# A two-layer attention and GLA trunk: other orders of sums, squares, copies and loads at the beginning, at the MLP starts and at the end of layer 0's attention

## The chip, the cores and the metric

The kernel runs on one core of a Trainium2 chip. The metric is the device time of one execution in microseconds (us). A core has a matrix engine (TensorE, PE in the profile, with its weight loads as PEld), a vector engine (VectorE, DVE), an activation engine (ScalarE, ACT), GpSimd (POOL) and a queue engine (SyncE, SP) that issues nearly all DMAs here. Every engine works off its own instructions strictly in the order in which the program lists them, and waits on semaphores for the others. So an order written in the program is an order of execution on that engine.

## The reference

Input and output are (1, 1024, 1024) float32: 1024 rows (S), width D = 1024, two layers.

```python
for i in range(DEPTH):
    h = rmsnorm(x, norm_mix_w[i])
    x = x + (dilated_attention if i == 0 else gla_mixer)(h, ...)
    h = rmsnorm(x, norm_mlp_w[i])
    x = x + sq_relu_mlp(h, mlp_w_up[i], mlp_w_down[i])     # relu(h @ w_up)**2 @ w_down, D_FF = 4096
return rmsnorm(x, final_norm_w)
```

Dilated attention has 8 heads of width 128 in three groups (window 128, 512, 2048; dilation 1, 4, 16), each group with its own q, k, v (h @ w_in, 9 x 1024 columns), rotary positions and a banded softmax; the three groups of a head are merged by their softmax denominators, and the merged rows go through w_out. GLA is chunked gated linear attention with 4 heads; the change does not touch it.

## The kernel before, in words

**Operands.** A float32 product is done by three matmuls in a reduced type: each operand x is cut into a high part h (an ACT copy) and a low part l = x - h (a DVE subtraction), and hi*hi, hi*lo, lo*hi are added in PSUM. A tile's name ends in h or l accordingly (`dh`/`dl`, `a12h`/`a12l`, `wgh`/`wgl`, `whi`/`wlo`).

**Seven products.** The large products (values, heads, up and down projections) split both matrices into 2 x 2 quarters and form seven products of quarters instead of eight. On the side of the activations, with a11, a12, a21, a22 the quarters of the transposed, normalised rows, the operands are a11, a12, a22, s1 = a21 + a22, s2 = s1 - a11, s3 = a11 - a21, s4 = a12 - s2. On the side of the weights they are quarters b and differences of them (tiles `t`, cut into `wb` and `wg`; `wa` and `wd` are plain quarters).

**Halves** (L338) makes the activations' operands from x: `norm` (row scale by `row_rstd`: ACT squares with a row sum, Ln and Exp on ACT with some small DVE steps; then `xn`, four or eight scalar_tensor_tensor steps on DVE), `turn` (PE transposes into a bank pT, ACT copies into the tile `a`), `sum1` to `sum4` (DVE), and `cut`/`split` (ACT copy, DVE subtraction). p = 0 to 3 is a block of 256 rows; c = 0, 1 is a half of an operand.

**The beginning** (from L1157) interleaves Halves with the first steps of `Values` (L700), which projects h onto v: step n has a `load`, a `prep` (perhaps a difference of weights, tile `kept`, then `dh` and `dl`), a `product` into four banks of pA or of pB, and `sums`, which empties banks (ACT copies `c<-pB`, DVE additions `c<-pA,c`). Steps 0 and 1 take a12 into pB, 2 and 3 a11 into pA, 4 and 5 s1 into pB, 6 and 7 s2 into pA, which needs pA emptied by `sums(4)` (blocks 0 and 1 of the four) and `sums(5)` (blocks 2 and 3). Two of the `dl` subtractions (`prep(0, pool)` and `prep(2, pool)`) run on POOL.

**The end of the attention** (from L1261): a queue of closures in time steps (`at(step, fn)`); the last head's scores (pS, on DVE and ACT the masked exponentials `pt`, the turned `pP`, the values `pO`) follow the last products of the head and run into the output projection. `follow` gives the steps at which each of the last heads' parts run, `tail` the merges of the last heads (`load`, `start`, `finish` make `om` from `rows`; `t_head` transposes them), `W.dma`/`W.prep` load and cut the output weights (`raw`, `whi`, `wlo`). `out_proj` (L1306) adds the projection to x block by block: a bank `pd` of 12 matmuls, then on DVE `xs<-pd,xs`; after each it advances the queue.

**The MLP start.** `out_proj` calls `Halves.middle` and `Halves.after` between its last blocks, then `Halves.finish` (L440), an order written out by hand of the up projection's products (`up.product(p, s)`) with everything else. `Up` (L520) has 16 pairs p of 256 columns; `load` brings a pair's weights, `stage(p, 0..6)` makes its operands, `done` reads a bank after its product and squares the result, `sums` forms what the down projection needs. s = 0 to 6 stands for a11, a12, s2, s1, s3, a22, s4. Banks X, Y, Z, V are shared: (p, s2) and (p, s3) add to X after (p, a11). From p = 2 or 3 on `Up.run` goes on in a regular order. Both layers have the same start.

## Time and profile before

| what | us |
|---|---|
| median of 3 runs | 2719.67 (2719.61 to 2720.84) |
| profiled execution, its own time | 2720.89 |
| its span in the profile | 2719.1 |
| PE busy | 2647.2 (97%) |
| DVE / ACT / POOL busy | 1790.9 / 1236.9 / 97.3 |
| mean granted PE clock | 0.991 |

The span is cut into stretches in the prediction: the beginning is 0 to 80 us, layer 0's attention ends and the output projection runs from 880 to 1004 us, layer 0's MLP starts at 1004 us and layer 1's at 2080 us. A row of the timeline gives start, duration, engine, line, operation, out<-in, shapes, count, and in brackets the idle time before it with what ended it. A row of the waits view gives the engine, what waited, for what, the total us, how many times and the longest.

### The profile page before, as it was taken

The page shows a single profiled execution, that of the slowest core. Times are in us where ns is not written, and L with a number is a line of the kernel's source. Part 1 is how long each engine was busy: PE and PEld are TensorE (multiplying, and loading weights), DVE is VectorE, ACT ScalarE, POOL GpSimd, SP SyncE. Part 2 cuts the span into 40 slices and gives each one's busy share as a digit, 9 for nine tenths or more (in the row PEclk, how much of TensorE's full clock was granted, in tenths as well). Part 3 has the DMA queues.
Part 4 walks back from the last instruction along what each step waited for, and adds up shares of the span by engine and source line. Part 5 has one row for each costly group of instructions (what it writes and reads, how often), then busy time and mean ns, then how long its engine had stood idle before and what let it go on. Part 6 is the DMA issues. An engine that isn't in the chain of part 4 may idle for free.

```text
span 2719.1 us, 33226 instructions
## 1 busy us (share of the span) xinstructions
PE 2647.2 (97%) x12248; PEld 2185.8 (80%) x12248; DVE 1790.9 (66%) x2938; ACT 1236.9 (45%) x2296; POOL 97.3 (4%) x74
## 2 busy tenths in 40 slices
PE   7999999999999898999999999999999899999998
PEld 5788888888888786888888887778888688888887
DVE  5744788888888667666656672562657766656567
ACT  5423355555555345555534343442425555553344
POOL 0000000000000000000000001321200000000000
PEclk9999999999999999999999999999999999999999
DMA  3542455655656533444775453012223444486543
GB/s 144 170 148 92 125 140 145 163 148 139 164 135 190 193 116 111 165 145 154 268 253 191 132 179 113 24 36 66 80 92 117 139 151 151 151 311 211 194 145 126
DMA packets 311412, 402.16 MB, mean 148 GB/s; under 512 B 18865, under 2 KB 183217, under 8 KB 311249
## 3 DMA queue, kind: packets, MB, share of 16 engines
q1 hardware_dynamic: 311248, 400.04, 46.6%
q8 instruction: 96, 1.57, 0.2%
q14 instruction: 68, 0.55, 0.1%
HBM read 267.13 MB, written 107.68 MB: 138 GB/s over the span
## 4 chain that ended last, share of the span: by engine, by line
PE 58%; DVE 6%; ACT 3%; issue 1%; DMA 0%; SPq 0%; DVEq 0%; ACTq 0%
PE pB L1439 13%; PE pA L1439 10%; PE pX L613 7%; PE pd L213 5%; PE pd L215 5%; PE pd L214 5%; PE pV L613 5%; PE pZ L613 2%; PE pY L613 2%; PE pT L263 1%; PE pO L1614 1%; PE pU L1600 0%; PE pO L1613 0%; PE pT L363 0%; ACT c L622 0%
## 5 line engine op out<-in xcount | busy, mean ns | idle before, releaser
L1439 PE MATMUL pB<-dh 128*128 128x512 f32 x512 | 199.4, 389 | 0.0
L1439 PE MATMUL pB<-dh,dl 128*128 128x512 f32 x512 | 199.2, 389 | 0.0
L1439 PE MATMUL pB<-dl,dh 128*128 128x512 f32 x512 | 199.2, 389 | 0.0
L222 DVE TENSOR_TENSOR dl<-sin,dh 128x1024 fp32r<-128x1024 f32 x112 | 136.6, 1220 | 43.4 <-ACT dh L219 42.8
L219 ACT ACTIVATE dh<-sin 128x1024 fp32r<-128x1024 f32 x112 | 117.8, 1052 | 89.2 <-PE pB L1439 38.6
L872 ACT ACTIVATE pt<-pt,orow 128x128 f32<-128x128 f32 (+1 forms) x192 | 85.0, 444 | 151.8 <-DVE orow L870 150.8
L613 PE MATMUL pV<-s4h,wd 128*128 128x512 f32 x448 | 152.1, 400 | 1.1 <-DVE rb L640 1.1
L219 ACT ACTIVATE dh<-kept 128x1024 fp32r<-128x1024 f32 x64 | 67.9, 1061 | 183.1 <-DVE kept L1404 137.8
L1439 PE MATMUL pA<-dh 128*128 128x512 f32 x384 | 149.4, 389 | 0.0
L1439 PE MATMUL pA<-dl,dh 128*128 128x512 f32 x384 | 149.4, 389 | 0.0
L1439 PE MATMUL pA<-dh,dl 128*128 128x512 f32 x384 | 149.4, 389 | 0.0
L551 DVE TENSOR_TENSOR wbl<-t,wbh 128x1024 fp32r<-128x1024 f32 x56 | 68.6, 1225 | 71.5 <-ACT wbh L550 71.5
L613 PE MATMUL pX<-s3h,wgh 128*128 128x512 f32 x224 | 94.8, 423 | 18.5 <-ACT wgh L550 11.9
L1439 PEld LDWEIGHTS pB<-dh,dl 128*128 128x128 f32 x512 | 96.1, 188 | 20.0
L1439 PEld LDWEIGHTS pB<-dl,dh 128*128 128x128 f32 x512 | 96.1, 188 | 19.9
L1439 PEld LDWEIGHTS pB<-dh 128*128 128x128 f32 x512 | 96.1, 188 | 19.8
L622 ACT ACTIVATE c<-c 128x512 f32<-128x512 f32 x64 | 40.5, 632 | 147.3 <-DVE c L632 97.2
L551 DVE TENSOR_TENSOR wal<-raw,wah 128x512 fp32r<-128x512 f32 (+1 forms) x108 | 76.1, 706 | 44.8 <-ACT wah L550 44.8
L148 POOL TENSOR_TENSOR wlo<-raw,whi 128x1024 fp32r<-128x1024 f32 x16 | 40.0, 2499 | 1759.1 <-ACT whi L147 1756.1
L613 PEld LDWEIGHTS pV<-s4h,wd 128*128 128x128 f32 x448 | 84.1, 188 | 20.5 <-DVE rb L640 2.8
L213 PE MATMUL pd<-whi,hTh 128*128 128x512 f32 x256 | 100.5, 393 | 0.0
L215 PE MATMUL pd<-whi,hTl 128*128 128x512 f32 x256 | 99.7, 389 | 0.0
(309 smaller groups left out, 7479.1 us busy)
## 6 DMA issues: line engine op xcount, KB each, us to landing
sin<-acts SPq DMA_DIRECT2D x112, 512.0 KB, 3.7
raw<-in_mlp_w_up_dram SPq DMA_DIRECT2D x64, 512.0 KB, 6.1
acts<-s SPq DMA_DIRECT2D x64, 512.0 KB, 3.3
raw<-in_mlp_w_down_dram SPq DMA_DIRECT2D x64, 512.0 KB, 4.6
raw<-in_attn_w_in_dram SPq DMA_DIRECT2D x96, 256.0 KB, 4.4
cw<-c SPq DMA_DIRECT2D x192, 128.0 KB, 2.3
acts<-c SPq DMA_DIRECT2D x64, 256.0 KB, 2.0
kept<-in_mlp_w_down_dram SPq DMA_DIRECT2D x32, 512.0 KB, 5.2
```

What stands on the lines that cost most here:

```text
L148: eng.tensor_tensor(lo, src, hi.bitcast(F32), op=OP.subtract)
L213: pe.matmul(ps, sh, mh, start=start, stop=False)
L214: pe.matmul(ps, sh, ml, start=False, stop=False)
L215: pe.matmul(ps, sl, mh, start=False, stop=stop)
L219: act.activation(hi, src, AF.Copy)
L222: dve.tensor_tensor(lo, src, hi.bitcast(F32), op=OP.subtract)
L263: pe.transpose(ps[:, k, 128 * i:128 * i + 128], src(k, i), ident)
L551: self.remain(lambda: dve.tensor_tensor(lo, src, hi.bitcast(F32), op=OP.subtract))
L613: pe.matmul(st[b], u[:, k, :], v, start=first and k + n == 0, stop=k == 3 and n == 2, skip_group_check=True)
L622: act.activation(r, r, AF.Relu)
L872: act.activation(pt[:, i, :128 * n], pt[:, i, :128 * n], AF.Exp, scale=-1.0, bias=m, accum_out=self.row[:, r, HD:HD + 1])
L1439: pe.matmul(self.acc[s][t], a[:, k, c], b[:, k, :], start=fresh and m + k + v == 0, stop=m == 7 and k == 1 and v == 2, skip_group_check=True)
```

## The change

The operations stay the same; two subtractions change their engine. In four places instructions are put into another order:

- **The beginning.** `prep` is divided into `total`, `rounded` and `remain`, so that a weight difference, its high part and its low part can stand apart. Block 0's transposes come as pairs (2, 3), a12's cut, then (0, 1). POOL's two subtractions move to DVE. `norm(2)` and the row scale of block 3 come before block 1's transposes, `norm(3)` before the second halves of products 0 and 1, `sum1` and the cuts of s1 half by half. `sums(4)` and `sums(5)` come later.
- **The end of layer 0's attention.** `Turned` owns the tiles xs and can load them, which it does for two row blocks during the last head. The output weights' loads, cuts and the transposes of the merged rows get other steps; the last head's parts follow at other steps, and the queue is advanced three times at the tail's start instead of once.
- **Both MLP starts** (the same code). The up weights are loaded one block of the output projection earlier and cut earlier; `first_weights` uses other tiles; `done` is divided into `add` and `squared`. The products come in the order (0,s2) (0,s1) (1,s2) (1,s1) (0,s3) (0,a22) (1,s3) (1,a22) (2,s2) (2,s1) (0,s4) (1,s4) (2,s3) (2,a22) (2,s4) (3,s2); before, it was (0,s2) (0,s1) (1,s2) (1,s1) (0,s3) (0,a22) (0,s4) (1,s3) (1,a22) (1,s4) (2,s2) (2,s1) (2,s3) (2,a22) (2,s4) (3,s2).

At the beginning, DVE's rows from the last low part of s2 to sum4. Before (`c_419`, `c_421` are the blocks 2 and 3 of pA, that is `sums(5)`; `a<-a,s_454` is sum4):

```order
L375 TENSOR_TENSOR s2l<-s_455,s2h 128x2x256
L779 TENSOR_TENSOR c_419<-pA,c_419 128x512
L779 TENSOR_TENSOR c_421<-pA,c_421 128x512
L730 TENSOR_TENSOR kept<-raw,kept 128x1024
L749 TENSOR_TENSOR dl<-kept,dh 128x1024
L730 TENSOR_TENSOR kept<-raw,kept 128x1024
L749 TENSOR_TENSOR dl<-kept,dh 128x1024
L379 TENSOR_TENSOR a<-a,s_454 128x2x256
L379 TENSOR_TENSOR a<-a,s_455 128x2x256
L379 TENSOR_TENSOR a<-a,s_454 128x2x256
L379 TENSOR_TENSOR a<-a,s_455 128x2x256
```

and now (`c_441`, `c_443` are `sums(4)`, `c_445`, `c_447` are `sums(5)`):

```order
L378 TENSOR_TENSOR s2l<-s_394,s2h 128x2x256
L801 TENSOR_TENSOR dl<-kept,dh 128x1024
L771 TENSOR_TENSOR kept<-raw,kept 128x1024
L831 TENSOR_TENSOR c_441<-pA,c_441 128x512
L831 TENSOR_TENSOR c_443<-pA,c_443 128x512
L801 TENSOR_TENSOR dl<-kept,dh 128x1024
L382 TENSOR_TENSOR a<-a,s_393 128x2x256
L382 TENSOR_TENSOR a<-a,s_394 128x2x256
L382 TENSOR_TENSOR a<-a,s_393 128x2x256
L382 TENSOR_TENSOR a<-a,s_394 128x2x256
L831 TENSOR_TENSOR c_445<-pA,c_445 128x512
L831 TENSOR_TENSOR c_447<-pA,c_447 128x512
```

The additions that empty pA's blocks 2 and 3 stood ahead of the weights of steps 6 and 7; now they stand behind both, and behind the four pieces of sum4.

At the start of the output projection, PE's rows from the last head's last scores to the first block. Before:

```order
L856 MATMUL pS<-kT,qT 128x128
L856 MATMUL pS<-kT,qT 128x256
L883 MATMUL pP<-ident,pt 128x128 x3
L897 MATMUL pO<-v,pt 128x128 x3
L213 MATMUL pd<-whi,oTh 128x512
L214 MATMUL pd<-wlo,oTh 128x512
L215 MATMUL pd<-whi,oTl 128x512
```

and now:

```order
L908 MATMUL pS<-kT,qT 128x128
L908 MATMUL pS<-kT,qT 128x256
L935 MATMUL pP<-ident,pt 128x128 x3
L949 MATMUL pO<-v,pt 128x128 x3
L935 MATMUL pP<-ident,pt 128x128 x3
L949 MATMUL pO<-v,pt 128x128 x3
L213 MATMUL pd<-whi,oTh 128x512
L214 MATMUL pd<-wlo,oTh 128x512
```

One more set of turned exponentials (pP) and of their values (pO) stands ahead of the first block of the projection; it stood behind that block.

At the MLP start of layer 0, DVE's rows from s3's operand to sum4. Before:

```order
L379 TENSOR_TENSOR a<-a 128x4x256 x2
L632 TENSOR_TENSOR c_8974<-pY,e_8945 128x512
L375 TENSOR_TENSOR s3l<-a,s3h 128x2x256 x4
L632 TENSOR_TENSOR c_8990<-pY,e_8988 128x512
L587 TENSOR_TENSOR t<-raw 128x512
L588 TENSOR_TENSOR t<-raw,t 128x512
L375 TENSOR_TENSOR a22l<-a,a22h 128x4x256 x2
L551 TENSOR_TENSOR wgl<-t,wgh 128x1024
L551 TENSOR_TENSOR wd<-raw,wd 128x512
L379 TENSOR_TENSOR a<-a,s_8728 128x2x256
L379 TENSOR_TENSOR a<-a,s_8729 128x2x256
L379 TENSOR_TENSOR a<-a,s_8728 128x2x256
```

and now:

```order
L382 TENSOR_TENSOR a<-a 128x4x256 x2
L603 TENSOR_TENSOR t<-raw 128x512
L604 TENSOR_TENSOR t<-raw,t 128x512
L378 TENSOR_TENSOR s3l<-a,s3h 128x2x256 x4
L567 TENSOR_TENSOR wgl<-t,wgh 128x1024
L567 TENSOR_TENSOR wd<-raw,wd 128x512
L666 TENSOR_TENSOR c_9023<-pY,e_8966 128x512
L378 TENSOR_TENSOR a22l<-a,a22h 128x4x256 x2
L603 TENSOR_TENSOR t<-raw 128x512
L604 TENSOR_TENSOR t<-raw,t 128x512
L382 TENSOR_TENSOR a<-a,s_8732 128x2x256
L382 TENSOR_TENSOR a<-a,s_8733 128x2x256
```

The difference t (L603, L604) from which wg of pair 0 is made has moved ahead of s3's low part, and wg's own low part ahead of that of a22; the t of pair 1 has moved ahead of sum4.

The diff, without the parts that only hand names on:

```diff
@@ -339,23 +339,26 @@
-def turn(self, p):
-    if p % 2 == 0:
+def turn(self, p, pairs=(0, 2, 1, 3)):
+    if p % 2 == 0 and (p // 2, 0) not in self.a:
         for k in range(2):
             self.a[p // 2, k] = self.one("a", F32)
-    xn = self.xn.pop(p)
-    for kp in (0, 2, 1, 3):
+    xn = self.xn[p]
+    for kp in pairs:
@@ -417,24 +420,27 @@
         self.split("a12", self.a[0, 1], 1, self.one, self.one)
     elif tb == 7:
         self.turn(2)
-        self.up.stage(1, 0)
-        self.up.stage(1, 1)
 
 def after(self, tb):
+    up = self.up
     if tb == 7:
         self.sum1(0)
     if tb % 2:
         self.norm(tb // 2)
-    if tb == 2:
-        self.up.load(0)
+    if tb == 1:
+        up.load(0)
+    elif tb == 2:
+        up.load(1)
+    elif tb == 3:
+        up.stage(0, 0)
+        up.stage(0, 1)
     elif tb == 4:
-        self.up.load(1)
+        up.stage(1, 0)
+        up.stage(1, 1)
+        up.first_weights(2)
+        up.first_weights(3)
     elif tb == 5:
-        self.up.stage(0, 0)
-    elif tb == 6:
-        self.up.stage(0, 1)
-        self.up.first_weights(2)
-        self.up.first_weights(3)
+        up.stage(0, 2)
 
 def finish(self):
     up, a = self.up, self.a
@@ -445,73 +451,78 @@
             self.split(name, src, c, self.one, lo)
 
     up.product(0, P1)
-    up.product(0, P2)
     self.sum2(0)
     up.done(0, P1)
     up.first_stage(2)
-    up.stage(0, 2)
-    up.first_stage(3)
+    up.product(0, P2)
     up.stage(0, 3)
     up.product(1, P1)
     self.turn(3)
+    up.first_stage(3)
     up.product(1, P2)
     up.product(2, P1)
     up.product(2, P2)
     up.product(3, P1)
     up.product(3, P2)
+    up.done(1, P1)
     self.sum1(1)
     self.sum2(1)
-    up.done(1, P1)
     split("s2", self.s2, self.two)
-    up.done(0, P2)
-    up.done(1, P2)
+    up.add(0, P2)
+    up.add(1, P2)
+    up.done(2, P1)
+    split("s1", self.s1, self.one)
+    up.squared(0, P2)
     up.stage(1, 2)
-    split("s1", self.s1, self.one)
     up.stage(1, 3)
-    up.done(2, P1)
+    up.squared(1, P2)
     up.product(0, P6)
-    for c in range(2):
-        self.combine(c, a[1, 0], a[0, 0], a[1, 0], OP.subtract)
+    up.add(2, P2)
+    up.done(3, P1)
+    self.sum3()
+    up.squared(2, P2)
+    up.stage(0, 4)
     up.product(0, P5)
-    up.done(2, P2)
     split("s3", a[1, 0], self.two)
-    up.done(3, P1)
-    up.done(3, P2)
-    up.stage(0, 4)
-    up.product(1, P6)
     up.done(0, P6)
-    split("a22", a[1, 1], self.one)
     up.stage(0, 5)
     up.stage(0, 6)
     up.load(2)
+    up.product(1, P6)
+    up.add(3, P2)
+    split("a22", a[1, 1], self.one)
+    up.done(1, P6)
+    up.squared(3, P2)
+    up.stage(1, 4)
     up.product(1, P5)
-    up.done(0, P5)
+    self.sum4()
+    up.stage(1, 5)
     up.product(0, P7)
-    up.done(1, P6)
-    for c in range(2):
-        self.combine(c, a[0, 1], a[0, 1], self.s2, OP.subtract)
-    up.product(0, P4)
     up.done(0, P7)
     split("s4", a[0, 1], self.two)
-    up.done(1, P5)
-    up.stage(1, 4)
-    up.done(0, P4)
-    up.stage(1, 5)
-    up.product(0, P3)
+    up.product(0, P4)
     up.stage(1, 6)
     up.load(3)
+    up.add(0, P4)
     up.product(1, P7)
+    up.done(1, P7)
     up.stage(2, 2)
-    up.done(0, P3)
     up.stage(2, 3)
+    up.squared(0, P4)
     up.product(1, P4)
-    up.done(1, P7)
-    up.sums(0)
+    up.add(1, P4)
+    up.product(2, P6)
     up.stage(2, 4)
-    up.product(1, P3)
-    up.done(1, P4)
+    up.squared(1, P4)
+    up.done(2, P6)
+    up.product(2, P5)
     up.stage(2, 5)
     up.stage(2, 6)
+    up.product(0, P3)
+    up.product(1, P3)
+    up.add(0, P3)
+    up.squared(0, P3)
+    up.sums(0)
 
     NP = FF // 256
     ORDER = ("a12", "a11", "s1", "s2", "s4", "s3", "a22")
@@ -676,10 +710,13 @@
                 self.load(p + 2)
             if s > first:
                 self.done(p, s - 1)
-            if p > 2 or s > 1:
+            if p == 2:
+                for t in ((2, 3), (4, 5), (6,))[s - 4]:
+                    self.stage(p + 1, t)
+            else:
                 self.stage(p + 1, s)
-            if p == 3 and s < 4:
-                self.stage(p + 1, s - 2)
+                if p == 3 and s < 4:
+                    self.stage(p + 1, s - 2)
             if p == NP - 1:
                 tail(s)
     self.h.clear()
@@ -744,9 +785,20 @@
-    hi, lo = k4([P, 2, 512], F32R, "dh"), k4([P, 2, 512], F32R, "dl")
+    self.t[n] = t
+
+def rounded(self, n):
+    if n not in self.t:
+        self.total(n)
+    t = self.t.pop(n)
+    hi = k4([P, 2, 512], F32R, "dh")
     act.activation(hi, t, AF.Copy)
-    eng.tensor_tensor(lo, t, hi.bitcast(F32), op=OP.subtract)
+    self.cut[n] = hi, t
+
+def remain(self, n):
+    hi, t = self.cut[n]
+    lo = k4([P, 2, 512], F32R, "dl")
+    dve.tensor_tensor(lo, t, hi.bitcast(F32), op=OP.subtract)
     self.cut[n] = hi, lo
@@ -1157,51 +1209,59 @@
 sp.dma_start(masks, msk)
 hs = Halves(x0, wbc, vals, False)
 hs.norm(0, 256)
-vals.prep(0, pool)
-hs.turn(0)
+vals.rounded(0)
+hs.turn(0, (2, 3))
+vals.remain(0)
+hs.cut("a12", 0)
+hs.turn(0, (0, 1))
 vals.prep(1)
-hs.cut("a12", 0)
-vals.prep(2, pool)
 hs.cut("a11", 0)
+vals.prep(2)
 vals.prep(3)
 hs.norm(1)
-for n in range(4):
+for n in range(3):
     vals.product(n, [0, 1])
+hs.norm(2)
+hs.rstd(3)
 hs.turn(1)
+vals.product(3, [0, 1])
 hs.cut("a12", 1)
 hs.cut("a11", 1)
-hs.norm(2)
+hs.turn(2)
+hs.norm(3)
+vals.load(4)
+vals.load(5)
 for n in range(2):
     vals.product(n, [2, 3])
-vals.load(4)
-vals.load(5)
-hs.turn(2)
-hs.norm(3)
-for n in range(2, 4):
-    vals.product(n, [2, 3])
+hs.sum1(0)
+vals.total(4)
+hs.cut("s1", 0)
+vals.total(5)
+hs.turn(3)
+vals.product(2, [2, 3])
 vals.sums(2)
 vals.sums(3)
 vals.prep(4)
-hs.turn(3)
-for c in range(2):
-    hs.sum1(c)
-for c in range(2):
-    hs.cut("s1", c)
+hs.sum1(1)
+hs.cut("s1", 1)
 vals.prep(5)
+vals.product(3, [2, 3])
 vals.load(6)
 vals.load(7)
-vals.sums(4)
+for c in range(2):
+    hs.sum2(c)
+vals.total(6)
+for c in range(2):
+    hs.cut("s2", c)
 vals.load(8)
 vals.product(4)
-for c in range(2):
-    hs.sum2(c)
-for c in range(2):
-    hs.cut("s2", c)
-vals.sums(5)
 vals.prep(6)
-vals.product(5)
+vals.total(7)
+vals.sums(4)
 vals.prep(7)
 hs.sum4()
+vals.sums(5)
+vals.product(5)
 for c in range(2):
     hs.cut("s4", c)
 hs.sum3()
@@ -1263,13 +1329,14 @@
     for k in range(0, KT, 2):
         add_rows(a_out, k)
     c = 14 * p
-    at(c + 2, lambda: (W.dma(), ol.extend(ahead_h8(0))))
-    for i in range(3):
-        at(c + 4 + 2 * i, lambda: W.dma())
-    for i in range(4):
-        at(c + 8 + 2 * i - (i == 3), lambda: W.prep(dve), 7)
-    at(c + 9, lambda: turned.turn(0), 7)
-    at(c + 11, lambda: (turned.turn(1), ol.extend(ahead_h8(1))), 7)
+    at(c + 3, lambda: (W.dma(), ol.extend(ahead_h8(0))))
+    for t in (4, 6, 7):
+        at(c + t, lambda: W.dma())
+    for t in (6, 8, 9, 11):
+        at(c + t, lambda: W.prep(dve), 7)
+    at(c + 7, lambda: turned.turn(0), 7)
+    at(c + 9, lambda: (turned.load_x(0), turned.load_x(1)))
+    at(c + 10, lambda: (turned.turn(1), ol.extend(ahead_h8(1))), 7)
 heads.run_head(p)
 
     def drain_to(mark):
@@ -1281,10 +1348,11 @@
 def tail():
 
     c = clock[0]
-    heads.follow(heads.count - 1, c - 1, ((7, 9, 11, 13), (10, 12, 14, 16), (12, 14, 16, 18)))
+    heads.follow(heads.count - 1, c, ((7, 8, 9, 10), (10, 11, 12, 13), (12, 13, 14, 15)))
     load, start, finish = merges(HEADS - 1, merged)
     rows = {}
-    advance()
+    for _ in range(3):
+        advance()
 
     def early(half):
         t = rows[half] = h8([P, 4, 512], F32, "ol2")
@@ -1293,22 +1361,18 @@
-    at(c + 18, lambda: (load(0), load(1)), 9)
-    at(c + 23, lambda: start(0))
-    at(c + 24, lambda: finish(0))
-    at(c + 25, lambda: start(1))
-    at(c + 27, lambda: finish(1))
+    at(c + 16, lambda: (load(0), load(1)), 9)
+    at(c + 21, lambda: start(0))
+    at(c + 22, lambda: finish(0))
+    at(c + 23, lambda: start(1))
+    at(c + 24, lambda: finish(1))
     steps.extend([advance] * 40)
```

## The prediction, made before the changed kernel ran

> **What bounds the kernel now.** I read the engine totals first, then the table by stretches of time, then what TensorE (PE) waited for. The columns of the table are the stretch, its length, busy time and instruction count of PE, of its weight loads, VectorE (DVE), ScalarE (ACT) and GpSimd (POOL), then the granted clock, the DMA share and GB/s.

> ```profile
> PE 2647.2 (97%) x12248; PEld 2185.8 (80%) x12248; DVE 1790.9 (66%) x2938; ACT 1236.9 (45%) x2296; POOL 97.3 (4%) x74
> ...
> 0.00:80.00 80.00, 57.76 (x222) 43.57 (x223) 47.95 (x76) 38.69 (x65) 5.33 (x6) 0.91 0.42 148
> 80.00:880.00 800.00, 798.42 (x4004) 672.39 (x4003) 606.00 (x1165) 392.31 (x960) 0.00 (x0) 1.00 0.53 146
> 880.00:920.00 40.00, 33.39 (x181) 28.25 (x180) 24.47 (x62) 17.34 (x55) 0.00 (x0) 0.96 0.81 259
> 1000.00:1080.00 80.00, 69.35 (x296) 55.09 (x295) 62.71 (x94) 44.01 (x67) 0.00 (x0) 0.94 0.25 88
> 2120.00:2160.00 40.00, 32.97 (x127) 25.33 (x126) 28.03 (x41) 17.24 (x22) 0.00 (x0) 0.92 0.36 123
> ```

> PE is busy 97% of the time and wholly busy between 80 and 880 us. An order that only moves other engines' work can gain nothing there. It can gain where PE is idle or slow: the first 80 us (call it A), the end of layer 0's attention (B, 880 to 950) and the two MLP starts (C, 1005 to 1085; D, 2080 to 2160). These are the places that the diff touches. PE's own list of waits says which are large (total us, times, longest):

> ```profile
> PE pX L613 <- ACT wgh L550: 11.9, 4, 3.2
> PE pX L613 <- ACT e L618: 7.0, 4, 3.3
> PE pS L856 <- DVE qT L967: 5.5, 3, 4.7
> PE pB L764 <- ACT a12h L373: 4.5, 2, 2.6
> PE pB L764 <- ACT s1h L373: 3.3, 1, 3.3
> PE pd L214 <- DVE wlo L148: 3.1, 4, 1.8
> PE pT L1097 <- DVE om L1054: 1.5, 1, 1.5
> ```

> A wait costs more than its length, because the clock often falls after it:

> ```profile
> 57.70:64.80 7.10, 6.28 (x15) 4.47 (x16) 5.98 (x9) 2.83 (x4) 0.00 (x0) 0.53 0.00 0
> 78.20:87.70 9.50, 9.50 (x42) 7.84 (x41) 9.50 (x13) 6.66 (x9) 0.00 (x0) 0.98 0.31 101
> 1042.00:1048.00 6.00, 5.58 (x12) 3.94 (x13) 4.57 (x7) 0.93 (x2) 0.00 (x0) 0.51 0.85 280
> 1057.20:1062.30 5.10, 4.51 (x12) 3.34 (x13) 3.72 (x5) 1.77 (x5) 0.00 (x0) 0.67 0.13 47
> 1076.90:1079.80 2.90, 2.87 (x12) 2.36 (x13) 2.87 (x5) 0.92 (x1) 0.00 (x0) 1.00 0.64 239
> ```

> At full clock 42 matmuls of 128x512 take 9.50 us, so 0.226 us each and 2.72 us for a product of 12. After the waits at 1042 and 1057 the 12 take 6.0 and 5.1 us; after the one at 1077, 2.9 us. So a wait of about 3 us costs between 0 and 3.3 us more.

> **The change, part by part. A, the beginning.**

> ```profile
> 17.15 0.80 PE L764 MATMUL pB<-dh,a12h 128*128 128x512 f32 x1 [2.58 <-ACT a12h L373]
> 44.82 1.15 PE L363 MATMUL pT<-ident,xn 128*128 128x128 f32 x8 [0.25 <-ACT a L365]
> 8.26 5.36 DVE L256 SCALAR_TENSOR_TENSOR xn<-x,y,wbc 128x256 f32<-128x256 f32 x8
> 24.39 2.74 DVE L256 SCALAR_TENSOR_TENSOR xn<-x,y,wbc 128x512 f32<-128x512 f32 x4
> 10.48 2.46 POOL L749 TENSOR_TENSOR dl<-raw,dh 128x1024 fp32r<-128x1024 f32 x1 [10.04 <-ACT dh L748]
> 19.84 1.04 ACT L243 ACTIVATE junk<-x 128x1024 bf16<-128x1024 f32 x1
> 8.80:87.71 78.91, 65.47 (x257) 49.96 (x257) 54.30 (x80) 41.37 (x67) 5.12 (x2) 0.91 0.36 128
> 50.17:81.42 31.25, 24.55 (x93) 18.64 (x92) 26.62 (x37) 13.19 (x20) 0.00 (x0) 0.84 0.26 85
> ```

> From PE's first transpose to the first s4 product it does 192 matmuls (43.4 us) and 64 transposes (8 in 1.15 us, so at most 9.2): of 78.91 us some 27 are lost. The eight xn steps took 5.36 us, though 256 columns should take half of the 0.69 us of 512 (2.74 for four) and a fixed part, about 0.48; one of them overlapped POOL's subtraction. That subtraction now goes to DVE (1.22 us, after the xn steps), so xn ends about 1.6 us earlier; and the transposes that feed a12 come first, with a12's copy before those of a11. Laying ACT's and DVE's durations into the new order, the first product starts near 14.3 instead of 17.15. Then a price: four squares of 1.04 us for blocks 2 and 3, and the row scale of block 3, now stand on ACT ahead of turn(1)'s copies. DVE reaches xn(1) near 22.8 (24.39 before), xn(2) ends near 29.7, the scale near 30.2; a12's second half comes to 34.7, and PE waits from 30 to 34.9. After that block 3's normalisation does not stall PE any more, since xn(3) starts near 35.8, not 50.17. From there until the last c<-pA addition DVE has the same instructions as before had from 50.17 to 81.42: 26.6 us busy. Added to 35.8 with 5 us of waiting for turn(3)'s copies, the last addition ends near 67.4. It frees the banks that the third block of s2's product writes; it now stands behind sum4 (the order of both is shown in the section on the change), and that is the new wait: PE, through s1 at 60.9, does 6 matmuls of s2, stops near 63.9 for 3.4 us, then has 42 left, 9.5 us, and about 2 us of slow clock. s2 ends near 78.9, not 87.71. **A: 8.8, taken as 8.5 us**; 5 if DVE's waits double, 10.5 if PE's wait is hidden.

> **B, the end of attention.**

> ```profile
> 897.19 0.69 DVE L1330 TENSOR_TENSOR xs<-pd,xs 128x512 f32<-128x512 f32 x1 [2.05 <-DMA xs<-in_x_dram]
> 904.55 1.22 PE L856 MATMUL pS<-kT,qT 128*128 128x128 f32 x4 [4.69 <-DVE qT L967]
> 932.82 2.36 DVE L148 TENSOR_TENSOR wlo<-raw,whi 128x1024 fp32r<-128x1024 f32 x2 [0.25 <-ACT whi L147]
> 941.31 1.76 DVE L1060 TENSOR_TENSOR rows<-rows,me 128x1536 f32<-128x1536 f32 x1
> 944.58 0.66 PE L1097 MATMUL pT<-ident,om 128*128 128x128 f32 x4 [1.55 <-DVE om L1054]
> ```

> The first loads of xs move into the last head, so DVE's 2.05 us for a DMA goes, and with it most of the 4.69 us in which PE waits for qT behind it; the weights' cuts come two steps earlier, so the short waits for whi and wlo go. Together up to 7 us. Against it: the queue of the last head is advanced three times instead of once before the first projection block. On PE a second set of pP and pO now stands before that block and waits for an exponential that ACT can only start when DVE has read the scores: about 3.5 us, and 2 us remain before pS. Later, om comes two blocks (5.4 us) earlier on PE, but its DVE chain (about 1.0 of small steps, 1.76, two of 0.69) now has both wlo (2.36) ahead of it. Chain minus one block of 2.72 gives a wait near 4, and near 1.9 for the second om, where there was 1.55. Gain 7, loss 5.5 + 4.3, less 1.3 for slow clock behind the 4.69 (taken between the 0 and 3.3 above): **B costs 1.5 us**, between a gain of 5 (nothing new waits) and a cost of 5 (each new wait also slows the clock).

> **C and D, the MLP starts.**

> ```profile
> 1041.98 0.79 PE L613 MATMUL pX<-s3h,wgh 128*128 128x512 f32 x1 [3.19 <-ACT wgh L550]
> 1057.26 0.50 PE L613 MATMUL pX<-s3h,wgh 128*128 128x512 f32 x1 [2.76 <-ACT wgh L550]
> 1076.93 0.50 PE L613 MATMUL pX<-s3h,wgh 128*128 128x512 f32 x1 [3.27 <-ACT e L618]
> 1036.59 0.68 DVE L632 TENSOR_TENSOR c<-pY,e 128x512 f32<-128x512 f32 x1
> 1063.30 1.22 DVE L551 TENSOR_TENSOR wbl<-t,wbh 128x1024 fp32r<-128x1024 f32 x1 [2.31 <-ACT wbh L550]
> 1027.74:1064.52 36.78, 29.40 (x107) 22.20 (x106) 24.84 (x35) 18.47 (x25) 0.00 (x0) 0.86 0.25 86
> 1038.62:1085.24 46.62, 35.97 (x133) 27.16 (x133) 32.34 (x45) 22.02 (x28) 0.00 (x0) 0.89 0.41 140
> 2113.85:2160.47 46.62, 35.48 (x136) 26.75 (x135) 32.59 (x46) 22.41 (x29) 0.00 (x0) 0.93 0.42 140
> ```

> From the end of (1,s1) at 1038.62 to (3,s2) at 1085.24 PE has 11 products, 29.9 us: 16.7 are lost, in layer 1 to the hundredth the same. Three waits (9.2 us) and the slow clock behind them make most of it. In the new order wg's operand of pair 0 is built ahead of s3's remainder, so (0,s3) starts at 1038.62 without a wait, and wg of pair 1 just about in time ((1,s3) at 1044.1 waits 0.7). What paces then is DVE. From the last s1l to pair 2's wbl it was busy 24.8 us of 36.8; the new order puts the two steps of t for pair 1 into this stretch (about 1.3 us), and if it runs without gaps pair 2's wbl ends at 1027.7 + 26.1 = 1053.8. PE has done four products by 1038.62 + 0.7 + 10.9 = 1050.2: a wait of 3. Six products later, near 1070, (2,s4) needs rb(2), which on DVE stands behind c12(1), the two steps of t, wbl and the four sums of pair 1. These begin when (1,s4) ends, near 1064.6: c12 takes 0.7, ACT's two squarings and the copy of wbh some 2.8 by its 1.04 for 1024 columns, wbl 1.2, the four sums and rb 0.6 to 0.7 each, so it ends near 1072.5: a wait of 2.4, with all later products behind it. Together 1038.62 + 29.9 + 0.7 + 3 + 2.4 + 1 of slow clock = 1075.7. The up weights are asked for one block of the projection earlier on SP, so they land no later than before; a load of x's rows that they are put ahead of there can come later by at most their two transfers. **C and D: 9.5 us each**; 13 if DVE's pieces overlap the products, 6 if DVE leaves as many gaps as in one of the old waits.

> Sum: 8.5 + 9.5 + 9.5 - 1.5 = 26. The span was 2719.1, the profiled execution 2720.9, 1.2 above the median of 2719.67. The span becomes 2693 and the median 2693.7, so **2694**.

> What a slow clock costs decides some 4 us of it. In the rows above the wait of 3.27 us was followed by a clock of 1.00 and that of 2.76 by 0.67, so length alone does not tell. [...]

> **Rivals.** (1) Almost all stalls vanish, because DVE runs ahead: its busy time in C was 32.3 of 46.6. A 10.5, C and D 13 each, B 4: 2679. Against it: the strings above have few gaps to give. (2) The stalls only change place: DVE's or ACT's order leaves gaps of the old size (11.9 of 36.8 us in that stretch), so C and D give 5 each, A 6, B costs 2: 2706. (3) No slow clock follows the shorter waits: the 2 us in A and 1 each in C and D go, 2690. [...] (4) Slower: in B every one of the eight row blocks of the output projection waits for DVE to read its pd bank, because rotary steps and the exponentials' scores now stand ahead in DVE's queue; at 4.69 us each, 37.5 us, it passes the 27.5 of the rest: 2730. It decides from 3.4 us per block; against it, DVE was busy only 24.5 of the 40 us there. (5) The order binds nothing, since products wait for transfers: 2720; against it, only one wait above names a DMA.

> **How the numbers follow.** The forecast has 0.50; (1) 0.14, (2) 0.19, (3) 0.08, (4) 0.06, (5) 0.03. All parts at their bounds would give 2678 (10.5 + 26 + 5 gained) to 2708 (5 + 12 - 5); they hardly all err to one side, so the forecast's own range is 2686 to 2702. With (1) and (2) it reaches 2680 to 2708, and no more than 2 in 10 is left out. 0.2% is about 5.4 us, what this kernel's times can tell from no change: faster 0.91, same 0.03, slower 0.06.

> **What would show it.** Right: first pB near 14.3; s2's third block waits about 3 us for c<-pA; (0,s3) has no wait, (2,s2) waits for wbl, (2,s4) for rb; no qT wait over 3 us in B, but om waits of 4 and 2. Wrong: the (3,s2) products less than 6 us earlier relative to (1,s1); an idle PE between xs and pd in B; a new wait that names a DMA.

## The result, and the profile after

The changed kernel takes 2703.14 us (median of 4, 2702.78 to 2703.76) against 2720.07 us: 16.9 us or 0.6% less, ratio 0.9938 with an interval of 0.992 to 0.9955. Timed again in a later comparison it took 2700.26 against 2720.25, ratio 0.9926 (0.9911 to 0.9942). So the gain lies between 17 and 20 us, where 26 were forecast. The sign was right, and the time lies in the range of 2680 to 2708; of the forecast's own narrower range, 2686 to 2702, the first median lies 1 us outside and the second inside. Besides POOL's two subtractions, four cuts of the up weights changed their form: they are done in halves, so the page counts 6 more instructions on DVE and 4 more on ACT.

PE's waits in the changed kernel (total us, times, longest):

```profile
PE pT L366 <- DVE xn L256: 11.5, 4, 10.8
PE pV L629 <- DVE rb L654: 6.3, 4, 2.6
PE pA L816 <- DVE c L831: 4.0, 2, 3.0
PE pX L629 <- ACT wbh L566: 3.9, 2, 1.9
PE pP L935 <- ACT pt L924: 3.7, 1, 3.7
PE pT L1149 <- DVE mz L1088: 3.5, 1, 3.5
...
PE pT L263 <- DMA ol<-oscr: 1.1, 1, 1.1
PE pS L908 <- DVE qT L1019: 1.1, 3, 0.4
```

Of the large waits of before, the one for xn at the start stays (10.1 us then); the others are gone or small (wgh 11.9, e 7.0, qT 5.5, a12h 4.5, s1h 3.3 before; e 1.4 and qT 1.1 now). New ones stand in their place: c<-pA, pt, the merge that makes om (mz is a small step of it), wbh, rb, and one that names a DMA. Where they stand, in PE's timeline:

```profile
10.80 3.86 PE L366 MATMUL pT<-ident,xn 128*128 128x128 f32 x16 [10.80 <-DVE xn L256]
67.08 0.80 PE L816 MATMUL pA<-dh,s2h 128*128 128x512 f32 x1 [3.04 <-DVE c L831]
864.26 1.06 PE L263 MATMUL pT<-ident,ol 128*128 128x128 f32 x8 [1.14 <-DMA ol<-oscr]
883.77 1.18 PE L935 MATMUL pP<-ident,pt 128*128 128x128 f32 x3 [3.72 <-ACT pt L924]
932.01 0.63 PE L1149 MATMUL pT<-ident,om 128*128 128x128 f32 x4 [3.54 <-DVE mz L1088]
1046.61 0.50 PE L629 MATMUL pX<-s2h,wbh 128*128 128x512 f32 x1 [1.93 <-ACT wbh L566]
1066.60 0.79 PE L629 MATMUL pV<-s4h,wd 128*128 128x512 f32 x1 [2.57 <-DVE rb L654]
2137.51 0.50 PE L629 MATMUL pV<-s4h,wd 128*128 128x512 f32 x1 [2.57 <-DVE rb L654]
```

The stretches behind some of them, and both MLP stretches that the prediction costed, from the end of (1,s1) to (3,s2):

```profile
67.08:73.00 5.92, 5.92 (x14) 4.72 (x15) 5.92 (x8) 4.08 (x6) 0.00 (x0) 0.50 0.80 265
932.00:936.90 4.90, 4.89 (x17) 3.58 (x18) 4.69 (x10) 1.19 (x3) 0.00 (x0) 0.65 0.00 0
1033.10:1071.02 37.92, 32.66 (x134) 25.63 (x132) 29.62 (x43) 17.60 (x23) 0.00 (x0) 0.95 0.40 135
1066.60:1071.00 4.40, 4.40 (x12) 3.52 (x13) 2.97 (x4) 1.33 (x2) 0.00 (x0) 0.62 0.96 305
2102.39:2141.95 39.56, 34.33 (x133) 26.80 (x132) 29.59 (x43) 17.63 (x23) 0.00 (x0) 0.91 0.38 131
```

Layer 0's MLP stretch fell from 46.62 to 37.92 us. Layer 1's fell from 46.2 to 39.56: by PE's timeline its (1,s1) ends at 2114.25 us in the kernel before, not at 2113.85, where the prediction let the stretch begin. After several of the new waits the granted clock is 0.5 to 0.65 for some us: behind the one for rb, 12 matmuls, 2.72 us at full clock, took 4.4.

To follow the time through all runs I cut each trace at PE instructions that every order has: the start of s4's first product (A); from the last s1 product of the heads that comes before the attention's end to the first up product (B); from the last s1 matmul of the MLP start to pair 4's first product (C and D); and the stretch between C and D, from that product to layer 1's first up product, in which every run has the same order on PE. The heads between A and B are in no column; they took 779 to 782 us, and 785 in the last two runs. All in us, read from PE's timelines, with the median of the runs:

| kernel | A | B | C | between | D | median |
|---|---|---|---|---|---|---|
| before | 87.7 | 135.5 | 61.4 | 980.0 | 61.0 | 2720.1 |
| changed | 79.6 | 138.7 | 53.5 | 981.6 | 55.1 | 2703.1 |
| only the beginning | 79.7 | 135.3 | 62.0 | 978.3 | 62.3 | 2709.6 |
| only the attention's end | 87.4 | 141.3 | 61.3 | 980.0 | 61.0 | 2725.4 |
| only the MLP starts | 86.6 | 136.4 | 54.8 | 981.6 | 55.0 | 2707.6 |
| changed, again | 78.6 | 140.4 | 53.5 | 981.6 | 55.1 | 2700.3 |
| one advance | 76.6 | 135.6 | 55.1 | 978.4 | 53.5 | 2699.0 |
| om later | 75.0 | 135.9 | 53.4 | 981.6 | 53.5 | 2698.3 |
| rb first | 76.6 | 141.2 | 53.9 | 981.2 | 55.8 | 2702.6 |
| additions first | 70.3 | 139.6 | 54.8 | 981.7 | 55.1 | 2698.2 |
| without the attention's part | 78.8 | 135.3 | 53.4 | 981.6 | 55.1 | 2697.2 |
| beginning and attention mended | 70.7 | 132.1 | 55.0 | 976.8 | 55.0 | 2692.7 |
| and the MLP starts | 70.9 | 132.3 | 54.4 | 975.8 | 51.5 | 2686.7 |

### The profile page after: what moved, and what is told of

It is laid out like the page before. It is cut to its first block, busy times and chain, and to the rows that moved or that the text cites. A ratio compares the mean times of both kernels' runs of the same rounds, so it can differ in the third digit from the quotient of the medians.

```text
span 2701.3 us, 33223 instructions
## 1 busy us (share of the span) xinstructions
PE 2642.5 (98%) x12248; PEld 2184.9 (81%) x12248; DVE 1788.8 (66%) x2944; ACT 1239.4 (46%) x2300; POOL 92.2 (3%) x72
## 4 chain that ended last, share of the span: by engine, by line
PE 59%; DVE 5%; ACT 2%; issue 1%; DVEq 0%; ACTq 0%
PE pB L1503 13%; PE pA L1503 10%; PE pX L629 8%; PE pd L213 5%; PE pd L215 5%; PE pd L214 5%; PE pV L629 5%; PE pZ L629 2%; PE pY L629 2%; PE pT L263 1%; PE pO L1678 1%; PE pU L1664 0%; PE pO L1677 0%; PE pT L366 0%; DVE wbl L567 0%
## 5 line engine op out<-in xcount | busy, mean ns | idle before, releaser
L567 DVE TENSOR_TENSOR wbl<-t,wbh 128x1024 fp32r<-128x1024 f32 x56 | 68.6, 1225 | 73.6 <-ACT wbh L566 73.6
L567 DVE TENSOR_TENSOR wal<-raw,wah 128x512 fp32r<-128x512 f32 x112 | 76.2, 687 | 47.7 <-ACT wah L566 47.7
L148 POOL TENSOR_TENSOR wlo<-raw,whi 128x1024 fp32r<-128x1024 f32 x16 | 40.0, 2499 | 1765.9 <-ACT whi L147 1762.9
L214 PE MATMUL pd<-wlo,hTh 128*128 128x512 f32 x256 | 99.6, 389 | 0.0
```

The costliest lines, as they stand in the source:

```text
L148: eng.tensor_tensor(lo, src, hi.bitcast(F32), op=OP.subtract)
L214: pe.matmul(ps, sh, ml, start=False, stop=False)
L567: self.remain(lambda: dve.tensor_tensor(lo, src, hi.bitcast(F32), op=OP.subtract))
```

## The experiments

**The parts alone.** Each is the kernel before with the diff's pieces for one place.

> Only the beginning is changed. Theory (the places add up): 8.1 us less than before, as the changed kernel's trace shows there (s4's first product at 79.6 instead of 87.7 us), so near 2712.0; the wait for c<-pA of about 3 us at 67 us is there too. Rival (a shift of everything after it moves where the clock falls): 8.1 plus or minus 1.5 to 3, because later waits that were followed by a slow clock no longer are, or the other way round.

> Only the end of layer 0's attention is changed. Theory (read from the changed kernel's trace): it costs 2.6 us, near 2722.6, with PE waits of 3.7 for pt and 3.5 for om. The forecast's step B: it costs 1.5, 2721.2. Rival: it gains by itself, up to 5 us (2715), and only loses in the changed kernel since the clock is slow there after the new waits.

> Only the two MLP starts are changed. Theory (read from the changed kernel's trace): 8.0 us less in layer 0 and 5.9 in layer 1, so near 2705.8, (2,s2) waiting for wb of pair 2 and (2,s4) for rb of pair 2 in both layers. The forecast's steps C and D: 19 us less, 2700.7. If the difference of 2 us between the layers is a matter of the clock alone, it need not come at the same layer here.

Measured against 2720.25 us: 2709.55 (ratio 0.9955, 0.994 to 0.997), 2725.42 (1.0017, 1.0008 to 1.0027) and 2707.64 (0.995, 0.9932 to 0.9967). So the beginning gives 10.7 us, the MLP starts 12.6, and the attention's end costs 5.2, more than the forecast's 1.5 and than the 2.6 that the first trace showed (3.2 in B, less 0.6 in the heads ahead of it). The sum, 18.1, agrees with the whole change's 17 to 20: the parts add up. Of the beginning's gain 8.0 us lie in A, as told; the other columns together gained nothing (between fell from 980.0 to 978.3, C and D rose by 0.6 and 1.3), so where the other 2.7 us lie is not shown. Changes of 0.6 to 1.7 us in stretches whose order stayed are what the rival named. With the MLP starts alone C and D took 54.8 and 55.0: the 2 us between the layers did not come in this kernel.

**The changed kernel once more.**

> The changed kernel once more, for the places of the slow clock. Theory (after the same wait the clock falls or does not fall by chance): the same median, near 2703.1, but in its trace the stretches with a granted clock under 0.7 are not all the same as in the first trace; above all the one at 1735 us, behind a wait of 2.05 us that the kernel before has too and passes at full clock. Rival (the clock follows from the order of the work): the same stretches, to a tenth of a us.

2700.26 us. The stretches with a clock under 0.7 came at nearly the same places, so for this pair the rival read it better; but the one at 68 us was half as long, and the four executions ran from 2699.99 to 2704.07. What the traces show of where the clock falls stands in the last section; the grid read there lay 0.83 us apart in the two traces, counted from the start of the span, of a step of 3.41, so the pair could not tell the two readings apart.

**The attention's end, two suspects.** First the queue's early advances:

```diff
-        for _ in range(3):
-            advance()
+        advance()
```

> The changed kernel, but the last head's queue is advanced once, not three times, ahead of the output projection, so that the second set of pP and pO stands behind the first block again. Theory (the three advances make most of what the end of the attention costs): PE's 3.7 us for pt and 0.6 for the values go, and the slow clock behind them (about 1 us); the stretch from the first s4 product to the first up product becomes 4 to 5 us shorter (919 to 921 now, so about 916), the time near 2697. Rival (the wait only moves): PE waits for qT or the scores some blocks later instead, as in the kernel before, and the time stays within 2 us of the changed kernel.

then the place of the merged rows' transposes:

```diff
-            at(clock[0] + 3, last)
+            at(clock[0] + 5, last)
```

> The changed kernel, but the transposes of the last head's merged rows (om) come two steps (one block) later. Theory: PE's wait of 3.5 us before om and the slow clock behind it (1.4 to 2.0 us) go, so about 5 us less, near 2697. Rival (om is late because DVE is): the wait shrinks by one block of 2.7 us at most, and what remains still slows the clock: 1 to 3 us less.

2698.95 us (0.9919, 0.9902 to 0.9935) and 2698.33 us (0.9914, 0.9899 to 0.9928). Either edit brings B back to 135.6 and 135.9 us, 3 to 5 us less than in the changed kernel. PE in the run with one advance:

```profile
881.49 0.33 PE L935 MATMUL pP<-ident,pt 128*128 128x128 f32 x1 [0.98 <-ACT pt L924]
...
892.56 0.68 PE L908 MATMUL pS<-kT,qT 128*128 128x128 f32 x4 [1.20 <-DVE qT L1019]
...
928.25 0.63 PE L1149 MATMUL pT<-ident,om 128*128 128x128 f32 x4 [2.31 <-DVE mz L1088]
```

The wait for pt fell from 3.72 to under 1 us at a time (2.7 in all), and that for qT came back with 1.2, not with the old 4.69; DVE's 2.0 us for the first loads of xs stay away, as in the changed kernel. In the run with om later 0.9 and 0.8 us are left of the waits at om, and the 3.7 for pt stays. By the stretch B both theories held; the medians, 1.3 to 4.8 us lower, would not tell them from their rivals alone.

**The MLP start, DVE's order.**

```diff
-                    elif s == first + 1:
+                    elif s == first + 1 and p > 2:
                         self.sums(p - 1)
                         self.load(p + 2)
                     if s > first:
                         self.done(p, s - 1)
+                    if p == 2 and s == first + 1:
+                        self.sums(p - 1)
+                        self.load(p + 2)
```

> The changed kernel, but at both MLP starts the four sums of pair 1 come behind rb of pair 2 on DVE. Theory (DVE's order sets the wait of (2,s4)): the wait of 2.57 us falls under 0.4 in both layers, with what slow clock follows it (1.7 us), so 3 to 4 us per layer and 6 to 8 in all, near 2695. Rival (DVE as a whole is late, its place does not matter): the wait comes back within two products at (3,s3) or (3,s4), and less than 3 us is gained in all.

2702.64 us, nothing gained, C and D as in the changed kernel. The waits view of that run says why:

```profile
PE pX L629 <- ACT e L634: 9.2, 2, 4.6
```

Both waits of 2.57 us for rb have gone, and one of 4.6 per layer stands at (3,s3): ACT's copy of X for pair 3 is queued behind the squares of pair 2, which wait for DVE. The rival was right: the wait moved.

**The beginning, DVE's order.**

```diff
-    vals.total(7)
     vals.sums(4)
+    vals.sums(5)
+    vals.total(7)
     vals.prep(7)
     hs.sum4()
-    vals.sums(5)
     vals.product(5)
```

> The changed kernel, but at the beginning both additions that empty pA's banks stand ahead of the weights of step 7 and of sum4 on DVE. Theory (the place of the additions behind sum4 makes PE's wait of 3.0 us): the wait at 67 us falls to under 0.5, the slow clock behind it (1.2 to 2.6 us) goes as well, s4's first product comes at 75 to 76 instead of 79.6: 3.5 to 5 us less, near 2698. Rival: the low part of step 7's weights, which now comes later, makes PE wait for it instead, and the gain is under 2 us.

2698.23 us (0.9917, 0.9902 to 0.9931). The wait at 67 us went, s4's first product came at 70.25, 4.7 to 9.4 us earlier than in the seven runs with the order of the change; some of it went into the wait that the rival named, in its timeline:

```profile
72.68 0.50 PE L816 MATMUL pB<-dl,s4h 128*128 128x512 f32 x1 [2.04 <-DVE dl L801]
```

**Putting it together.** The first is the changed kernel with the old attention's end. The second has the three edits that helped, and sum3 moved behind the low part for which PE waited:

```diff
-    hs.sum3()
     vals.load(9)
...
         if n == 6:
+            hs.sum3()
             for c in range(2):
                 hs.cut("s3", c)
```

The third has this in `Up.run` besides:

```diff
-                    if s == first:
+                    if p == 3 and s == first:
+                        self.done(p, s)
+                        self.squared(p - 1, 5)
+                        self.done(p - 1, 6)
+                    elif s == first:
                         self.done(p - 1, 6)
-                    elif s == first + 1:
+                    elif s == first + 1 and p > 2:
                         self.sums(p - 1)
                         self.load(p + 2)
-                    if s > first:
+                    if p == 2 and s == 6:
+                        self.add(p, 5)
+                    elif s > first and (p, s) != (3, first + 1):
                         self.done(p, s - 1)
+                    if p == 2 and s == first + 1:
+                        self.sums(p - 1)
+                        self.load(p + 2)
```

> The changed kernel with the end of layer 0's attention left as before; beginning and MLP starts changed. Theory (that part costs 4 us, as the stretch from there to the first up product shows: 135.4 to 136.4 us with the old order, 138.7 to 141.3 with the new): 4 us under the changed kernel, near 2697. The forecast's step B (it costs 1.5): 2699 to 2701.

> The changed kernel with the three edits that helped together (one advance, om one block later, pA's additions ahead of sum4), and sum3 moved behind the low part of step 8's weights, for which PE waited 2.0 us in the run with the additions first. Theory (the costs add up: about 4 for the additions and the slow clock behind their wait, 2 for that low part, 3 to 5 for each of the two edits at the attention's end): 2687 to 2692, the wait for pt, for om and for c<-pA all under 1 us, the stretch from the attention's end to the first up product near 132. Rival (the waits at the attention's end are one wait that moves): that stretch stays at 135 to 136 as with either edit alone, and the time is 2693 to 2696.

> As the run before, and at both MLP starts rb of pair 2 ahead of the sums of pair 1, and the copy of X for pair 3 ahead of the squares of pair 2 on ACT. Theory (two orders, on DVE and on ACT, made the two waits of 2.57 and 4.6 us; with both mended neither is left): both under 1 us, 3 to 4 us per layer less than the run before. Rival (DVE and ACT are both late there, and the wait moves on to a third place, (3,s4) or (4,a11)): less than 2 us per layer, or nothing.

2697.19 us (0.9916, 0.9899 to 0.9934), 2692.73 us (0.99, 0.9883 to 0.9917) and **2686.65 us (0.9884, 0.9865 to 0.9903)**, which beats the changed kernel by 14 to 16 us across comparisons and the kernel before by 35 in its own. The first bears out the cost of 3 to 6 us of the attention's part. In the second, B fell to 132.1: the two waits there were two, not one that moves. The time came out above the expected 2687 to 2692 all the same, since at the beginning a third wait came up in PE's timeline, now for a copy on ACT that empties a bank:

```profile
75.44 0.80 PE L816 MATMUL pB<-dh,s4h 128*128 128x512 f32 x1 [2.41 <-ACT c L826]
```

This wait came with the moved sum3. On ACT the copy stands behind the cut of s3, which waits for sum3, and it ended at 75.9 us, where it ended at 73.6 in the run with the additions first. From s4's first product to s3's PE took 16.0 us here, 13.2 in that run and 10.9 in the changed kernel. So moving sum3 removed most of the 2.0 us for the low part and still cost about 3.

In the third, layer 1's stretch fell to 51.5 and layer 0's hardly, and at (3,s4) of both layers a wait for rb came up, in layer 0:

```profile
1072.25 0.79 PE L629 MATMUL pV<-s4h,wd 128*128 128x512 f32 x1 [3.48 <-DVE rb L654]
```

In layer 1 it is 3.54 us. The two orders did make the two waits of 2.57 and 4.6, but PE's waits did not get less: from (2,s4) on they were 3.6 us in layer 0 and 3.7 in layer 1 in the run before. So the rival was right, DVE is late and the wait moves on. What layer 1 gained, 3.5 us, is slow clock but for 0.1 us: behind its 3.54 us, which ended at 2135.11, the clock did not fall, nor behind the wait of 1.94 us for wb ahead of it, which the edit does not touch and behind which the clock is 1.00 up to 2125 us. With four executions each, from 2688.86 to 2696.10 and from 2683.77 to 2691.42, it is not shown that the last 6 us come from this edit.

## Why the prediction was right or wrong

- **Where the time can be won** was right: the gain came at the beginning and at the MLP starts, and B, the fourth place, lost.
- **A, 8.5 us**: right. s4's first product came 8.1 us earlier in the first trace and 10.7 us were gained alone, 8.0 of them in A. The steps held one by one: the first product at 14.7 us (14.3 foreseen), the last c<-pA addition ended at 67.6 (67.4), the wait for it 3.0 (3.4). POOL's share was right too; the eight xn steps now take 3.26 us instead of 5.36. In the kernel before, seven of them took 0.48 us each and the one beside POOL's subtraction 2.58; now all eight take 0.48:

```profile
8.68 3.26 DVE L256 SCALAR_TENSOR_TENSOR xn<-x,y,wbc 128x256 f32<-128x256 f32 x8 [0.58 <-DMA wbc<-in_norm_mix_w_dram]
...
66.34 1.28 DVE L831 TENSOR_TENSOR c<-pA,c 128x512 f32<-128x512 f32 x2
```

- **B, a cost of 1.5 us**: the sign was right, the size was not; alone it cost 5.2. The wait for pt (3.5 foreseen, 3.72) and that for the first om (4, 3.54) came as told; the 2 us before pS and the second om's wait (1.9) did not come. By PE's timelines its waits in B add up to 9.5 us in the changed kernel and 8.7 before, 0.8 more where the sum had 2.8 more; the rest of the stretch grew by 2.3 us, where the sum had 1.3 less. So the step that failed is the slow clock: I let that of the old qT wait go and put none behind the new waits, though 932 to 936.9 us ran at 0.65. The two errors have opposite signs and partly hid each other. I had also not costed a wait for a DMA, which the prediction names as a sign of being wrong: for `ol`, whose load is issued one step later than before and whose first transposes stand two steps earlier. It was 1.14 us in the changed kernel, 0.5 to 2.6 in every run with the new attention's end, and absent in the four runs with the old; by the waits view of the run with that part alone:

```profile
PE pT L263 <- DMA ol<-oscr: 2.6, 1, 2.6
```

- **C and D, 9.5 us each**: the mechanism was right. Up to (3,s2), the stretch that I costed, C gave 8.7 us in the first trace, with the waits at wb (1.9 and 0.5, against 3) and rb (2.57, against 2.4) in the places foreseen; D gave 6.7 us, since the clock fell behind the wait for wb there and not in C. I took 1 us of slow clock for each stretch. By the rows above PE was busy 32.66 and 34.33 us with the 29.9 us of eleven products, 2.8 and 4.4 us more. The traces have one slow step of 3.41 us in C, from 1066.53, behind rb, and two in D, from 2117.84 and 2138.32, behind wb and rb; at half clock that makes 1.7 and 3.4 us. The other 1.0 or so is not clock, and the kernel before has it too (35.97 busy in C, with 10.24 us at half clock). And I stopped my sum at (3,s2): of the gain, 0.7 us per layer went back in the next products, where (3,s3) and (3,s4) wait about 0.5 us each. To pair 4 the gains are 7.4 us (C) and 6.8 (D), means over the eight traces with the new MLP orders and the three with the old.
- **Nothing elsewhere**: wrong by 1.6 us. In a stretch that the change does not touch, the clock fell after a wait that both kernels have (below).

Together: 1.1 to 3.7 us from B, some 2 to 2.7 in each MLP start, 1.6 between. Most of it is of one kind, slow clock after waits of 2 to 4 us, and the forecast's figure for it was too small in every place (in A 3.0 us came, not 2: the 42 matmuls behind the wait at 67 us took 12.5 us instead of 9.5). The waits for `ol`, at (3,s3) and at (3,s4) and the 1.0 us above in each MLP start are the rest. The prediction's upper figure for it, 3.3 us behind one wait, was too large where it was read: the rows of 6.0 and 5.1 us hold 0.4 and 0.6 us of a second wait.

Rival 3, no slow clock after the shorter waits, fell with the same rows. Rival 2, stalls that only change place, was right in part: at the beginning and the MLP starts each mended order brought up a next wait. The first median lies nearer to its 2706 than to 2694, but not by its terms: it gave C and D 5 us each and A 6. Of rival 4 nothing showed, PE waits for no bank that xs has to empty; rivals 1 and 5 are ruled out by the time.

## What to carry to other kernels

When engines are all near their limit, laying the measured durations into the new order engine by engine told most of the new waits here to about a us, and two that did not come; but behind a wait of 1.8 us or more the traces of the kernel before and of the changed kernel had none, one or two steps of 3.41 us at half clock, as the next section shows, so such a wait should be priced with another 0, up to 1.7 or up to 3.4 us, and the sum should run until the old rhythm is back, not to the first common point. Parts of a change that were made together should be timed apart: here one of three cost 5 us. After mending an order, look at once for the instruction that is late next, on whichever engine.

## What the runs showed of the hardware

Whether TensorE's clock fell after a wait of 2.0 to 2.1 us differed from trace to trace, with the same instructions and the same wait. In a part where no run changes PE's order, PE waits for kdT (2.08 us in the kernel before, 2.05 in the changed kernel, 2.04 in the run with beginning and attention mended). The stretch behind that wait, in the kernel before:

```profile
1748.35:1751.74 3.39, 3.35 (x17) 2.57 (x17) 1.48 (x3) 1.32 (x5) 1.96 (x3) 1.00 0.00 0
```

in the changed kernel:

```profile
1734.80:1739.77 4.97, 4.93 (x17) 3.70 (x17) 1.65 (x4) 2.43 (x7) 1.97 (x3) 0.66 0.00 0
```

and in the run with beginning and attention mended:

```profile
1725.58:1728.95 3.37, 3.33 (x16) 2.57 (x17) 1.46 (x3) 1.30 (x5) 1.96 (x3) 1.00 0.00 0
```

The same matmuls took 1.6 us longer in the changed kernel.

```profile
1744.25:1747.67 3.42, 2.06 (x10) 1.37 (x8) 3.31 (x3) 0.00 (x0) 3.42 (x2) 1.00 0.00 0
1747.67:1751.08 3.41, 2.69 (x14) 2.30 (x15) 1.89 (x3) 0.66 (x3) 2.07 (x4) 1.00 0.00 0
```

In the changed kernel the wait lies within one step, and the next step is slow:

```profile
1732.14:1735.55 3.41, 1.36 (x8) 0.88 (x7) 2.65 (x2) 0.00 (x0) 3.41 (x2) 1.00 0.00 0
1735.55:1738.97 3.42, 3.42 (x9) 2.63 (x8) 1.65 (x4) 2.09 (x7) 1.22 (x3) 0.50 0.00 0
1738.97:1742.38 3.41, 3.41 (x13) 1.97 (x12) 1.75 (x3) 1.73 (x4) 0.62 (x1) 1.00 0.00 0
```

PE's busy time in the step differs: 2.06 and 2.69 us in the first pair, 1.36 ahead of the slow step. Over the thirteen traces, 114 steps at full clock had PE busy for less than 47% of them, and 107 of these were followed by a slow step; of the other 9742 steps, 2 were. In the kernel before it was 10 of 11, and none of the other 746; in the changed kernel 10 of 10, and none of 747. A slow step was followed by full clock where PE was busy for 84% of it or more, else by another slow one; in these two traces the least with full clock behind it was 89%, the most with another slow one 81%. One slow step of 3.41 us at half clock does the work of 1.7 us, so it costs up to 1.7; for the matmuls behind kdT it was 1.6. The wait of 3.27 us at 1077 us that the prediction saw pass at full clock agrees with this: a line of the grid, at 1075.24, cut it in two, with PE busy 1.82 and 1.73 us of the two steps (53% and 51%). All this is read from the traces; no run shifted a wait against the grid on purpose, so that the busy share is the cause is not shown.

Such falls go with most of the difference with which the stretch between C and D took 975.8 to 981.6 us in the thirteen traces: 980.0 with two slow steps in the kernel before, 981.6 with three in the changed kernel, behind kdT, behind a wait of 1.9 us for AM and behind one of 1.8 for wlo. A, with the same code and the same wait of 3.0 us, took 75.0 to 79.7. In the run with om later, the clock did not fall at 36 us nor behind that wait:

```profile
36.00:40.00 4.00, 4.00 (x19) 3.27 (x19) 4.00 (x7) 1.21 (x3) 0.00 (x0) 1.00 0.16 22
62.00:68.00 6.00, 2.97 (x14) 2.24 (x13) 6.00 (x11) 4.03 (x5) 0.00 (x0) 1.00 0.47 147
```

The kernel before, in 14 executions on one chip, took 2716.7 to 2726.6 us. So single differences under some 3 us mean little here.
